# Loading all of x first and summing the adaptive columns in five groups

## The chip, the cores and the metric

The kernel runs on one core of one Trainium2 chip. The core has five engines with an instruction queue each: TensorE (PE; its weight loads are shown as PEld), VectorE (DVE), ScalarE (ACT), GpSimd (POOL) and SyncE (SP), which issues the DMAs. Each engine takes its own instructions strictly in the order in which they are written, and waits for the others through semaphores. The metric is the device time of one execution in microseconds. The times shown are the median of three runs.

## The reference, cut to what matters

Two layers of a decoder trunk run on x, 1024 rows (positions) by 1024 channels. Each layer begins with a norm of x that is scaled and shifted per channel, and then multiplies by the columns of a projection:

```python
c_act = jax.nn.silu(c)
for l in range(DEPTH):
    ada = c_act @ w_ada[l] + b_ada[l]
    shift, scale, gate = jnp.split(ada, 3, axis=-1)
    h = rmsnorm(x, norm_g[l]) * (1.0 + scale[:, None, :]) + shift[:, None, :]
    p = h @ w_in[l]
    ...                       # mLSTM heads and retention heads on the columns of p
    x = x + gate[:, None, :] * (concat(y_m, y_r) @ w_out[l])
return rmsnorm(x, final_g)
```

`w_ada[l]` is 1024 by 3072. The change touches layer 0 alone, and of it only what stands here up to the first columns of `p`.

## The kernel before, in words

Matrix products are made in three passes for accuracy: each operand is split into a rounded high part and a low part, and `mm3` (lines 144 to 147) multiplies high by high, low by high and high by low. So each 128 x 128 weight tile costs three matmuls of 512 columns for each half of the rows.

Everything ahead of the value projection of layer 0 is the first stage. It is written out by hand for all engines (lines 1052 to 1181), as a list of steps in a string, `script`; the kernel's scheduler takes over behind it for the engines other than TensorE, whose order is written throughout. The stage makes the products of the normed x with three column blocks of 128 (`firsts`), for 8 blocks of 128 channels (k) and 2 halves of 512 rows. Each pair (half, k) is a number n in `seq`, and passes through these steps:

- `T`: four transposes on TensorE of the scaled x (line 315) into one PSUM bank of the pool `pa`, which has four; one is kept for the adaptive sums and two, once in use, for the third weight's products, so that in most of the stage one is left for `T`
- `E`: evacuation with the channel's scale and shift (`gsh`), on ACT at line 321 or on VectorE at line 323
- `C`: the high part, a cast on ACT (line 1137)
- `U`: the low part, a subtraction on VectorE (line 1140)
- `F`: the nine matmuls with the three weights (lines 145 to 147)

The scale and the shift of a channel come out of `w_ada`. `ada_load` (line 232) loads a group of columns in eight pieces of 128 rows; step `A` (lines 244 and 246, VectorE) multiplies each piece by its entry of silu(c) and adds it up; step `P` (line 251, TensorE) sums over the partitions by four matmuls with a column of ones, each shown as two records; step `G` (lines 227 to 230, VectorE) makes `gsh` of them, with the columns of `norm_g` and `b_ada` that `ada_cols` (lines 193 to 199) has transposed on TensorE and copied on VectorE. There are four groups of 256 channels; a group's `E` waits for its `G`.

Of the other steps, `S` and `Q` are the squares of x's first and second half (ACT and VectorE in turn, lines 1072 and 1069) and, with `R`, the reciprocal root (POOL, line 1013); `N` and `X` scale the two halves (ACT line 308, VectorE line 310), step 0 for the first four channel blocks and steps 1 and 2 for the rest; `W` splits a weight (cast on ACT, line 614, subtraction at line 615: on POOL for the weights' first halves, `W00 W10 W20`, and on VectorE for the second); `D` multiplies a mask by itself on TensorE, and nobody reads the result (line 1151); `V` splits the weights of the value projection.

All loads are issued by SP in the order of lines 1082 to 1096. Eight semaphores take turns among the DMAs, so each issue waits until the DMA eight places ahead has landed. The order before is: c, the rows of `norm_g` and `b_ada`, adaptive group 0, x's first half, the first halves of three weights, x's second half, groups 1 and 2, the weights' second halves, group 3, then what comes later. `load_cact`, `ada_cols` and all of group 0's `A` stand ahead of the script.

Of the kernel before, what the change touches and what calls it, by code (L numbers as in the profile page):

```python
# [19 lines left out]
P = 128  # L20

D = 1024
# [58 lines left out]
def tile_hybrid_trunk(ctx, tc, x, c, positions, w_ada, b_ada, norm_g, w_in, conv_w, conv_b,  # L81
# [149 lines left out]

    def ada_load(l, g):
        raws = []
        for kk in range(KT):
            raw = bt()
            Q.dma_start(raw.rearrange("p (w c) -> p w c", w=2),
                        w_ada[l, kk * P:(kk + 1) * P].rearrange("p (w c) -> p w c", c=D)[:, 0:2, g * 256:(g + 1) * 256])
            raws.append(raw)
        return raws

    def ada_group(raws, acc, kks):
        for kk in kks:
            if kk == 0:
                V.tensor_scalar(acc, raws[0], cact[:, 0:1], None, ALU.mult)
            else:
                V.scalar_tensor_tensor(acc, raws[kk], cact[:, kk:kk + 1], acc, ALU.mult, ALU.add)

    def ada_sums(l, g, acc, pt):
        for which in range(2):
            for i in range(2):  # L250
                PE.matmul(pt[:, 4 * g + 2 * which + i:4 * g + 2 * which + i + 1],
                          acc[:, which * 256 + i * P:which * 256 + (i + 1) * P], ones, start=True, stop=True)
# [307 lines left out]
    def ocol(hg, m):  # L560
        return OFF_MO + hg * HD + m * P
# [537 lines left out]
    ada_cols(0, arows)  # L1099
    accs = [bt()]  # L1100
    ada_group(araw[0], accs[0], range(KT))
    pad = ps_a()

    for l in range(DEPTH):
# [8 lines left out]
        def first(half, k):  # L1113
            for i, w in enumerate(wf):
                if k == 0:
                    pf[i][half] = ps_p() if i < 2 else ps_a()
                half_block(pf[i][half], w, hT, half, k, k + 1)

        if l == 0:
            seq = [(half, k) for g in range(4) for half in range(2) for k in (2 * g, 2 * g + 1)]  # L1120
            w0, pts, hfs, rs1 = [], {}, {}, []
            script = ("P0 D6 S G0 W00 W10 N0 W20 T0 T1 E0 E1 C0 C1 U0 U1 F0 F1 Q R A102 X0 A124 T2 E2 C2 A146 T3 D3 E3 C3 U2 F2 "
# [4 lines left out]
            for step in script.split():  # L1127
# [4 lines left out]
                elif what == "E":  # L1132
                    hfs[n] = norm_evac(0, pts.pop(n), seq[n][1], n >= 2)
# [7 lines left out]
                elif what == "F":  # L1141
                    first(*seq[n])
                elif what == "A":
# [3 lines left out]
                    ada_group(araw[g], accs[g], range(a, b))  # L1147
                elif what == "D":
                    warm = ps_a()
# [4 lines left out]
                elif what == "G":  # L1154
                    finish_gsh(0, 2 * n, 2, pad[:, 4 * n:4 * n + 2], pad[:, 4 * n + 2:4 * n + 4])
# [21 lines left out]
                else:  # L1177
                    i, p = (int(d) for d in arg)
                    wf[i] += split_w(rw[i][p], P, V if p else G)
            head_cols(0, hrows)  # L1180
            startup.__exit__(None, None, None)
        else:
            for half in range(2):
                for k in range(KT):
                    first(half, k)
                    tick()
# [110 lines left out]
```

## Time and profile before

| | us |
|---|---|
| median of three runs | 2311.66 |
| lowest and highest | 2311.54, 2311.84 |
| the profiled execution's own time | 2311.88 |
| span of its records | 2310.0 |
| TensorE busy | 2277.8 (99%) |
| VectorE busy | 1353.2 (59%) |
| ACT busy | 907.1 (39%) |
| POOL busy | 823.5 (36%) |

How to read the lines below. In order of time: start, duration, engine, line, operation, output<-inputs, shape, x count of merged records; in brackets the idle time of that engine just before and what ended it. In a group of instructions: count | busy time, mean ns of one | idle time before them and what ended most of it. In a table of stretches: start and end, length, then busy time of each engine with the number of its instructions, the granted clock of TensorE as a share of full speed, the busy share of the DMA engines, and GB/s. A matmul on 32-bit floats (`T`, `P`, `D`, line 197) is shown as two records. The profile is of one execution.

### The profile page before, as it was taken

How to read it: one execution, taken by the hardware profiler on the slowest of the kernel's cores; microseconds unless marked ns; L12 is line 12 of the kernel's file. 1: busy time of each engine (PE TensorE's matmuls, PEld its weight loads, DVE VectorE, ACT ScalarE, POOL GpSimd, SP SyncE). 2: the span in 40 equal slices, each digit the busy share in tenths (PEclk: the TensorE clock that was granted, in tenths of full speed). 3: DMA queues.
4: the chain of work that ended last, by engine and by line, in shares of the span. 5: the costliest groups of instructions: out<-in, count | busy, mean ns of one | idle time of the engine just before them, and what ended most of it. 6: DMA issues, size and time to landing. Idle time of an engine off the chain costs nothing.

```text
span 2310.0 us, 34281 instructions
## 1 busy us (share of the span) xinstructions
PE 2277.8 (99%) x12447; PEld 1958.2 (85%) x12447; DVE 1353.2 (59%) x2835; ACT 907.1 (39%) x1768; POOL 823.5 (36%) x817
## 2 busy tenths in 40 slices
PE   7999999999999999999999999999999999999998
PEld 5888888889988888888888889888898888988886
DVE  7477688556555555584536665555563545556753
ACT  5535433444332323353434544344443323224442
POOL 1343424333343334222552434233334334341323
PEclk9999999999999999999999999999999999999999
DMA  8223232324433533486532322322323333436762
GB/s 257 80 64 98 73 84 80 82 74 116 120 109 88 150 83 87 128 258 217 177 92 57 84 72 77 84 74 69 81 70 89 81 87 93 124 81 205 240 231 78
DMA packets 328761, 259.44 MB, mean 112 GB/s; under 512 B 79732, under 2 KB 263804, under 8 KB 328592
## 3 DMA queue, kind: packets, MB, share of 16 engines
q1 hardware_dynamic: 328592, 257.27, 38.6%
q8 instruction: 97, 1.59, 0.3%
q14 instruction: 72, 0.59, 0.1%
HBM read 201.58 MB, written 55.61 MB: 111 GB/s over the span
## 4 chain that ended last, share of the span: by engine, by line
PE 91%; DVE 3%; DMA 3%; issue 1%; POOL 1%; ACT 1%; SPq 0%; POOLq 0%; DVEq 0%; ACTq 0%
PE pp L145 24%; PE pp L146 24%; PE pp L147 24%; PE pa L146 5%; PE pa L147 5%; PE pa L145 5%; PE pa L765 2%; DMA b<-in_w_ada_dram 1%; DMA b<-in_x_dram 1%; PE pa L315 0%; DMA raw<-in_w_ada_dram 0%; POOL wL L615 0%; POOL sL L615 0%; DVE b L266 0%; DMA b<-in_w_in_dram 0%
## 5 line engine op out<-in xcount | busy, mean ns | idle before, releaser
L145 PE MATMUL pp<-b,wH 128*128 128x512 f32 x1776 | 703.7, 396 | 1.1 <-ACT b L1137 1.1
L146 PE MATMUL pp<-b,wH 128*128 128x512 f32 x1776 | 700.2, 394 | 0.3 <-DVE b L1140 0.2
L147 PE MATMUL pp<-b,wL 128*128 128x512 f32 x1776 | 700.2, 394 | 0.0
L615 POOL TENSOR_TENSOR wL<-raw,wH 128x512 fp32r<-128x512 f32 x338 | 450.1, 1338 | 507.4 <-ACT wH L614 466.8
L147 PEld LDWEIGHTS pp<-b,wL 128*128 128x128 f32 x1776 | 333.9, 188 | 79.0
L146 PEld LDWEIGHTS pp<-b,wH 128*128 128x128 f32 x1776 | 334.2, 188 | 72.2 <-DVE b L1140 2.0
L145 PEld LDWEIGHTS pp<-b,wH 128*128 128x128 f32 x1776 | 334.4, 188 | 71.5 <-ACT b L1137 1.6
L614 ACT CAST wH<-raw 128x512 fp32r<-128x512 f32 x402 | 246.1, 616 | 322.8 <-PE pp L147 93.8
L145 PE MATMUL pp<-wH,b 128*128 128x256 f32 (+1 forms) x1152 | 353.0, 306 | 0.7 <-DVE g L543 0.7
L147 PE MATMUL pp<-wH,b 128*128 128x256 f32 (+1 forms) x1152 | 352.8, 306 | 0.0
L146 PE MATMUL pp<-wL,b 128*128 128x256 f32 (+1 forms) x1152 | 352.2, 306 | 0.0
L615 POOL TENSOR_TENSOR b<-acc,b 128x256 fp32r<-128x256 f32 (+1 forms) x208 | 200.8, 984 | 322.8 <-ACT b L614 315.2
L145 PEld LDWEIGHTS pp<-wH,b 128*128 128x128 f32 x1152 | 216.9, 188 | 12.3 <-DVE g L543 1.6
L147 PEld LDWEIGHTS pp<-wH,b 128*128 128x128 f32 x1152 | 216.6, 188 | 11.4
L146 PEld LDWEIGHTS pp<-wL,b 128*128 128x128 f32 x1152 | 216.7, 188 | 10.8
L632 DVE SCALAR_TENSOR_TENSOR acc<-pp,cols,acc 128x511 f32<-128x511 f32 (+2 forms) x192 | 142.5, 742 | 43.2 <-ACT acc L627 41.2
L614 ACT CAST b<-acc 128x256 fp32r<-128x256 f32 (+1 forms) x208 | 93.7, 487 | 187.4 <-DVE acc L709 127.6
L615 POOL TENSOR_TENSOR sL<-th,sH 128x384 fp32r<-128x384 f32 (+1 forms) x64 | 61.0, 953 | 236.5 <-ACT sH L614 171.9
L145 PE MATMUL pa<-wH,b 128*128 128x512 f32 x256 | 101.1, 395 | 0.0
L147 PE MATMUL pa<-wH,b 128*128 128x512 f32 x256 | 101.0, 394 | 0.0
L146 PE MATMUL pa<-wL,b 128*128 128x512 f32 x256 | 100.9, 394 | 0.0
L636 ACT ACTIVATE th<-acc 128x512 f32<-128x512 f32 x64 | 40.5, 632 | 146.3 <-DVE acc L634 79.3
(255 smaller groups left out, 3439.3 us busy)
## 6 DMA issues: line engine op xcount, KB each, us to landing
raw<-in_w_in_dram SPq DMA_DIRECT2D x274, 256.0 KB
raw<-in_w_out_dram SPq DMA_DIRECT2D x128, 256.0 KB
gdr<-g SPq DMA_DIRECT2D x64, 256.0 KB
ndr<-zt SPq DMA_DIRECT2D x128, 128.0 KB
raw<-in_w_ada_dram SPq DMA_DIRECT2D x64, 256.0 KB
g<-gdr SPq DMA_DIRECT2D x64, 256.0 KB
acc<-ndr SPq DMA_DIRECT2D x64, 256.0 KB
acc<-kdr SPq DMA_DIRECT2D x192, 64.0 KB
```

Of the source, the lines that this page charges most:

```text
L145: PE.matmul(o, lt[0], rt[0], start=start, stop=False)
L146: PE.matmul(o, lt[0], rt[1], start=False, stop=False)
L147: PE.matmul(o, lt[1], rt[0], start=False, stop=stop)
L614: A.copy(dst[0], src)
L615: eng.tensor_tensor(dst[1], src, f(dst[0]), ALU.subtract)
L632: V.scalar_tensor_tensor(acc[:, d:], pt[:, 0:HALF - d], wcol, acc[:, d:], ALU.mult, ALU.add)
L636: A.activation(th, acc, AF.Tanh, scale=0.5)
L765: PE.matmul(pd, kk[i][:, o:o + P], qd, start=dt == 0 and i == 0, stop=dt == 1 and i == 1)
```

## The change

The order of loads becomes: c, all of x, the rows of `norm_g` and `b_ada`, two weights' first halves, group 0, the third weight's first half, groups 1, 2 and 3, the weights' second halves, group 4. The groups are of 1, 1, 2, 2 and 2 blocks of 128 channels. For a group of one block, two pieces of `w_ada` share a buffer and are loaded by a DMA each, of half the size; its sums are over 256 columns instead of 512, and its `P` has two matmuls. The numbers n follow the groups: 0 and 1 are k = 0 of both halves, 2 and 3 are k = 1, and from 4 on they are as before.

The script is written anew. The squares and the scaling of both halves, two transposes and the warm-up multiplies (eight instead of six, and the later three go) stand ahead of `ada_cols`, now step `L`, and of group 0's `A`. For n = 0 and 1 the products with the first two weights (`f00 f01 f10 f11`) are written ahead of those with the third (`f02 f12`). A group's `A` is written about half a step earlier than before, and `P3 G3` ahead of `W01 W11 W21`. All weights are split on POOL, and all `E` run on ACT.

```diff
+    GROUPS = ((0, 1), (1, 1), (2, 2), (4, 2), (6, 2))
+
     def ada_load(l, g):
+        k, n = GROUPS[g]
         raws = []
-        for kk in range(KT):
+        for kk in range(0, KT, 3 - n):
             raw = bt()
-            Q.dma_start(raw.rearrange("p (w c) -> p w c", w=2),
-                        w_ada[l, kk * P:(kk + 1) * P].rearrange("p (w c) -> p w c", c=D)[:, 0:2, g * 256:(g + 1) * 256])
-            raws.append(raw)
+            for i in range(3 - n):
+                part = raw[:, i * 256:(i + 1) * 256] if n == 1 else raw
+                Q.dma_start(part.rearrange("p (w c) -> p w c", w=2),
+                            w_ada[l, (kk + i) * P:(kk + i + 1) * P].rearrange("p (w c) -> p w c", c=D)
+                            [:, 0:2, k * P:(k + n) * P])
+                raws.append(part)
         return raws
...
     Q.dma_start(crow[0:8, :], c[0].rearrange("(r c) -> r c", c=P))
+    xts = [load_x(0), load_x(1)]
     arows = load_ada_rows(0)
+    firsts = (zcol(0, 0), ocol(0, 0), zcol(0, 1))
+    rw = [[w_raw(col, 0)] for col in firsts[0:2]]
     araw = [ada_load(0, 0)]
-    xts = [load_x(0)]
-    firsts = (zcol(0, 0), ocol(0, 0), zcol(0, 1))
-    rw = [[w_raw(col, 0)] for col in firsts]
-    xts.append(load_x(1))
-    araw.append(ada_load(0, 1))
-    araw.append(ada_load(0, 2))
+    rw.append([w_raw(firsts[2], 0)])
+    araw += [ada_load(0, g) for g in (1, 2, 3)]
     for i, col in enumerate(firsts):
         rw[i].append(w_raw(col, 1))
-    araw.append(ada_load(0, 3))
+    araw.append(ada_load(0, 4))
...
     load_cact(crow)
-    ada_cols(0, arows)
-    accs = [bt()]
-    ada_group(araw[0], accs[0], range(KT))
+    accs = []
...
-            seq = [(half, k) for g in range(4) for half in range(2) for k in (2 * g, 2 * g + 1)]
-            script = ("P0 D6 S G0 W00 W10 N0 W20 T0 T1 E0 E1 C0 C1 U0 U1 F0 F1 Q R A102 X0 A124 T2 E2 C2 A146 T3 D3 E3 C3 U2 F2 "
-                      "A168 U3 P1 G1 N1 T4 F3 E4 C4 U4 N2 A202 T5 F4 E5 C5 U5 X1 A224 T6 F5 E6 C6 U6 X2 A246 T7 F6 E7 C7 "
-                      "A268 U7 W01 W11 W21 P2 G2 T8 F7 E8 C8 A302 U8 T9 F8 E9 C9 A324 U9 T10 F9 E10 C10 A346 U10 T11 F10 "
-                      "E11 C11 A368 U11 P3 G3 T12 F11 E12 C12 U12 T13 F12 V0 E13 C13 V1 U13 T14 F13 E14 C14 V2 U14 "
-                      "T15 F14 E15 C15 V3 U15 V4 F15 V5 V6 V7")
+            seq = [(half, k) for k0, n in GROUPS for half in range(2) for k in range(k0, k0 + n)]
+            script = ("S N0 T0 T2 D8 Q R L W00 W10 A003 X0 T1 A038 P0 G0 E0 C0 E1 C1 W20 A102 U0 f00 A124 f01 A146 U1 f10 f11 "
+                      "A168 P1 A201 G1 f02 f12 E2 C2 T3 E3 C3 A213 U2 N1 T4 F2 A236 A268 U3 P2 G2 F3 A302 N2 E4 C4 U4 "
+                      "T5 F4 E5 C5 A324 U5 X1 T6 F5 E6 C6 A346 U6 X2 T7 F6 E7 C7 A368 U7 P3 G3 W01 W11 W21 T8 F7 E8 C8 "
+                      "A402 U8 T9 F8 E9 C9 A424 U9 T10 F9 E10 C10 A446 U10 T11 F10 E11 C11 A468 U11 P4 G4 T12 F11 "
+                      "E12 C12 U12 T13 F12 V0 E13 C13 V1 U13 T14 F13 E14 C14 V2 U14 T15 F14 E15 C15 V3 U15 V4 F15 V5 V6 V7")
...
+                elif what == "f":
+                    first(*seq[n // 10], n % 10)
+                elif what == "L":
+                    ada_cols(0, arows)
...
-                    wf[i] += split_w(rw[i][p], P, V if p else G)
+                    wf[i] += split_w(rw[i][p], P)
```

In the script, `A124` is group 1's pieces 2 and 3; `f01` is n = 0 with weight 1; `D8` is eight warm-up multiplies.

More of the change, by code (lines that the diff above doesn't have):

```diff
@@ L248, in ada_sums @@
     def ada_sums(l, g, acc, pt):
+        k, n = GROUPS[g]
         for which in range(2):
-            for i in range(2):
-                PE.matmul(pt[:, 4 * g + 2 * which + i:4 * g + 2 * which + i + 1],
-                          acc[:, which * 256 + i * P:which * 256 + (i + 1) * P], ones, start=True, stop=True)
+            for i in range(n):
+                o = which * KT + k + i
+                PE.matmul(pt[:, o:o + 1], acc[:, (which * n + i) * P:(which * n + i + 1) * P], ones, start=True, stop=True)
     def ada_rows(l, c0, accs):
@@ L1141, in tile_hybrid_trunk @@
                 elif what == "F":
-                    first(*seq[n])
+                    for i in range(3):
+                        first(*seq[n], i)
+                elif what == "f":
+                    first(*seq[n // 10], n % 10)
+                elif what == "L":
+                    ada_cols(0, arows)
                 elif what == "A":
@@ L1184, in tile_hybrid_trunk @@
                 for k in range(KT):
-                    first(half, k)
+                    for i in range(len(wf)):
+                        first(half, k, i)
                     tick()
```

23 lines of the change are left out of this document (12 added, 11 removed).

## The prediction

> **What bounds the kernel now.** I read the page first, then busy time by stretch, then the first 74 us in order of time, by engine, with each wait. The stretches say where a gain can lie at all. Columns: PE, PEld, DVE, ACT, POOL busy (instructions), granted clock, DMA share, GB/s.
>
> ```profile
> span 2310.0 us, 34281 instructions
> 24.41:40.49 16.08, 15.57 (x65) 12.13 (x66) 12.82 (x30) 10.52 (x21) 1.19 (x1) 0.82 1.11 351
> 40.49:73.96 33.47, 32.49 (x167) 25.83 (x166) 22.82 (x39) 24.20 (x49) 6.62 (x12) 1.00 0.27 80
> 73.96:170.00 96.04, 96.04 (x515) 82.20 (x514) 58.32 (x117) 43.38 (x79) 37.70 (x38) 1.00 0.31 74
> 170.00:2300.00 2130.00, 2123.07 (x11669) 1830.51 (x11669) 1239.83 (x2611) 817.68 (x1599) 770.10 (x753) 1.00 0.38 110
> ```
>
> From 73.96 us on, where the first stage ends, TensorE is idle for 7 us in 2226. Nothing there gives slack back, so the end moves by as much as the first stage's end. All that counts is when TensorE finishes that stage. Its rows up to the first product, and the granted clock around it:
>
> ```profile
> 12.73 1.86 PE L251 MATMUL pa<-ones,b 128*128 128x1 f32 x8 [8.90 <-DVE b L246]
> 14.46 5.47 PE L1151 MATMUL pa<-rmask 128*128 128x256 f32 x12
> 22.52 0.77 PE L315 MATMUL pa<-ident,b 128*128 128x128 f32 x5 [0.97 <-DVE b L310]
> 24.41 0.79 PE L145 MATMUL pp<-b,wH 128*128 128x512 f32 x1 [1.12 <-ACT b L1137]
> 27.43 0.63 PE L145 MATMUL pa<-b,wH 128*128 128x512 f32 x1
> 27.86 0.63 PE L146 MATMUL pa<-b,wH 128*128 128x512 f32 x1
> 32.97 1.56 PE L1151 MATMUL pa<-rmask 128*128 128x256 f32 x6 [0.43 <-ACT acc L321]
> 36.80 0.95 PE L251 MATMUL pa<-ones,b 128*128 128x1 f32 x8
> 23.00:23.50 0.50, 0.29 (x3) 0.05 (x1) 0.50 (x1) 0.00 (x0) 0.50 (x1) 0.85 1.06 389
> 30.00:30.50 0.50, 0.50 (x3) 0.46 (x2) 0.37 (x2) 0.23 (x1) 0.24 (x1) 0.82 1.10 348
> ```
>
> The first product starts at 24.41. The clock is half from about 23.35 (0.85 over half a microsecond is 1.0 for 0.35 and 0.5 for 0.15) to 30.18 (0.82, in the same way): 6.83 us, two periods of 3.41. Counted back, further borders lie at 19.94, 16.52 and 13.11, and the next at 33.59. The warm-up multiplies of step D show as 12 records in 5.47 us at 14.46, 0.456 each, against 0.26 each at 32.97, so they ran slow to their end although the clock column says 1.00 there; I go by the durations. The full clock thus came at 19.94, just as they ended, and was lost at 23.35. [...]
>
> **The change, part by part.** *Loads.* The bytes are the same: group 0 and group 1 become 8 loads of 128 KB each, 512 bytes a piece, instead of 8 of 256 KB; 8 issues are added on SP's queue. The whole of x goes ahead of everything but c and the constants.
>
> ```profile
> 1.64 0.28 SPq L178 DMA_DIRECT2D rows<-in_norm_g_dram  x1
> 2.30 3.98 SPq L236 DMA_DIRECT2D b<-in_w_ada_dram  x8
> 5.08 0.49 DVE L244 TENSOR_SCALAR b<-b,cact 128x512 f32<-128x512 f32 x1 [0.96 <-DMA b<-in_w_ada_dram]
> 10.50:16.50 6.00, 3.77 (x13) 3.42 (x14) 4.01 (x9) 2.17 (x6) 0.00 (x0) 1.00 1.05 380
> 16.50:20.00 3.50, 3.42 (x9) 2.16 (x7) 1.80 (x10) 2.35 (x5) 1.49 (x2) 1.00 1.13 328
> 17.25 0.69 DVE L1069 SCALAR_TENSOR_TENSOR th<-b 128x512 f32<-128x512 f32 x1 [0.71 <-ACT th L1072]
> 19.57 1.33 ACT L308 ACTIVATE b<-b,rs 128x512 f32<-128x512 f32 x2
> ```
>
> x takes the place of the row at 1.64. The first load was used 2.78 us after its issue (2.30 to 5.08); the rest follow by 262 KB at 380 GB/s, 0.69 us, a little slower at the start, so 0.72: the eighth load of the first half lands at 1.64 + 2.78 + 7 x 0.72 = 9.5, the sixteenth at about 15. Two weight loads end near 16.7, group 0 (1.05 MB at the 328 GB/s of the stretch that has such 512-byte pieces in it) near 20, then a weight load, and group 1 near 25: SP issued eight in 3.98 us, so 0.5 each is its own bound. Groups 2 and 3 follow near 31 and 37, group 4 near 45. Each is there before it is asked for below, by 5 us or more for group 0's last load, so the smaller loads cost nothing; without that cover they would cost 16 x (0.5 - 0.4), under 2 us.
>
> *Ahead of the first product.* The order is now: norm of x's first half, two transposes T0 and T2, eight warm-up multiplies instead of six, then L, the transposition of the norm_g and b_ada rows, which in the kernel before stood ahead of all this. TensorE works in order, so L waits for all of D8; VectorE works in order too, and L's two copies stand ahead of all of group 0's sums, of the scaling X0 and of everything behind. This is the wait that the change adds. From the last square to the scaling took 2.32 us (17.25 to 19.57): here 9.5 to 11.8. Two scalings on ACT, 1.33, give 13.15; six transposes more (five took 0.77) end at 14.1. D8 is 16 records: 7.3 us at 0.456. At the border of 19.94, 12.8 of them are done; the other 3.2 at half the time end at **20.7**. From there the path is VectorE's:
>
> ```profile
> 3.54 0.28 PE L197 MATMUL pa<-ident,rows 32*128 32x32 f32 x1 [0.53 <-DMA rows<-in_b_ada_dram]
> 3.94 0.17 DVE L199 COPY cols<-pa 128x24 f32<-128x24 f32 x1
> L244 DVE TENSOR_SCALAR b<-b,cact 128x512 f32<-128x512 f32 x4 | 1.9, 482 | 1.0 <-DMA b<-in_w_ada_dram 1.0
> L246 DVE SCALAR_TENSOR_TENSOR b<-b,cact,b 128x512 f32<-128x512 f32 x28 | 21.0, 750 | 2.3 <-DMA b<-in_w_ada_dram 1.7
> L818 DVE SCALAR_TENSOR_TENSOR cf<-cf,pa 128x256 f32<-128x256 f32 x64 | 25.6, 401 | 0.0
> 30.27 0.88 DVE L310 TENSOR_SCALAR b<-b,rs 128x512 f32<-128x512 f32 x2
> 37.78 0.16 DVE L227 TENSOR_TENSOR gsh<-pa,cols 128x2 f32<-128x2 f32 x1 [0.94 <-PE pa L251]
> 38.30 0.78 ACT L321 ACTIVATE acc<-pa,gsh 128x512 f32<-128x512 f32 x1 [2.16 <-PE pa L315]
> 39.11 0.62 ACT L1137 CAST b<-acc 128x512 fp32r<-128x512 f32 x1
> 39.76 0.69 DVE L1140 TENSOR_TENSOR b<-acc,b 128x512 fp32r<-128x512 f32 x1 [1.56 <-ACT b L1137]
> ```
>
> L to its copies' end, 3.54 to 4.11: 0.57, so 21.3. Group 0 is one 128x256 TENSOR_SCALAR (0.28, a good half of 0.48) and seven 128x256 sums at 0.41 (the nearest row has 0.40; half of 0.75 is the lower end), with X0's two scalings, 0.88, among them: 4.0, so 25.3. Its sums on TensorE are four records at the slow 0.23 of the row at 12.73, since the clock is lost again at 23.35: 0.95, so 26.3. From there as from 37.78 to the end of the cast, 39.73: 1.95. The first product starts at **28.25**, 3.85 later than before, and TensorE is idle for some 6 of the 7.5 us ahead of it.
>
> *From the first product to the fifth step's (F4).* The products of group 0 use two weights; the third weight's come after group 1's sums. The second record of the first product waits for VectorE's 0.69, so 28.95; eleven at the slow 0.43 (27.43 to 27.86 above) end at 33.7, about when the border at 33.59 gives the clock back. Group 1's sums, small vectors and evacuation (0.5, 0.5, 0.8) end at 35.55, with the six products of the third weight beside them; T3, E3 and T4 wait for one another through one PSUM slot (0.45, 0.15, 0.8, 0.45), F2 runs from 37.5 to 39.6. VectorE has from 34.75 on two sums of group 2, one U, and five sums: 1.55 + 0.7 + 3.87, so 40.9; group 2's sums on TensorE wait for that, 1.3 us idle. F3 then ends at 43.85, T5 at 44.3. Before, 24.41 to 40.49 was 16.1; now 28.25 to 44.3 is 16.05: nothing won back. The warm-up D3 that went (1.56) is paid for by these waits.
>
> *From F4 to the stage's end.* The transposes mark the steps:
>
> ```profile
> 42.69 0.60 PE L315 MATMUL pa<-ident,b 128*128 128x128 f32 x4
> 45.21 0.60 PE L315 MATMUL pa<-ident,b 128*128 128x128 f32 x4
> 48.66 1.05 PE L251 MATMUL pa<-ones,b 128*128 128x1 f32 x8 [0.75 <-DVE b L246]
> 49.57 0.63 PE L315 MATMUL pa<-ident,b 128*128 128x128 f32 x4
> 52.27 0.66 PE L315 MATMUL pa<-ident,b 128*128 128x128 f32 x4
> 55.59 0.60 PE L315 MATMUL pa<-ident,b 128*128 128x128 f32 x4
> 49.12 1.89 DVE L615 TENSOR_TENSOR wL<-b,wH 128x512 fp32r<-128x512 f32 x3
> L615 POOL TENSOR_TENSOR wL<-raw,wH 128x512 fp32r<-128x512 f32 x338 | 450.1, 1338 | 507.4 <-ACT wH L614 466.8
> ```
>
> A step is 2.52 (42.69 to 45.21), nine products at 0.23 and four transposes; a group's sums (36.80) take 0.82 more, until the next transposes. Between 45.21 and 55.59 stand three steps and one such sum: 8.4, but they took 10.4. These 2.0 us were lost to group 2's last VectorE sums, to the three weight splits of 1.89 on VectorE and to the evacuation behind them. In the new order the next group's sums start half a step earlier and are reduced ahead of the splits, and the splits lie on POOL (three of 1.34, about 4 us, beginning some 2 us ahead of the first product that needs them, and the last needed 4 us later): I take the 2.0 as won. The rest, 33.47 - 2.0, brings the end from 44.3 to **75.8**, 1.8 behind 73.96. The first two evacuations move from VectorE to ACT, at 0.78 (38.30); VectorE's nearest row, U's 0.69, bounds what that costs at 0.1 each, and E1 lies beside the first products.
>
> Sum: +3.85 - 0.05 - 2.0 = +1.8 on the profiled execution's 2311.88, which stands 0.22 above the median: 2311.66 + 1.8 = **2313.5**. Unknown prices: D8's end between 18.9 and 21.4; the 2.0 won between 0.5 and 2.0.
>
> **Rivals.** [...]
>
> [...]
>
> *The loads decide (slower by over 0.2%).* If the 512-byte pieces of groups 0 and 1 move at a third of 328 GB/s, group 1 ends near 37 instead of 25, and its sums on TensorE, due at 33.7, come at 37.4: +3.7 more, **2317.2**. It decides from below 2.36 MB in the 16.5 us from 16.7 to 33.2, 145 GB/s; the stretch with such pieces shows 328.
>
> *The change does what its order suggests.* Were the rows' copies not behind D8, group 0 would be summed by 20.6 and the first product would start at 23.3 on a warm clock, with the 2.0 won as well: 23.3 + 42 us of TensorE work + 2.5 of waits = 67.8, **2305.5**. Against it: both engines keep their order.
>
> **How the numbers follow.** Forecast 0.5, earlier clock 0.25, slower clock 0.14, loads 0.05, no wait 0.06. The predicted time is the forecast's. The range from 2309.6 to 2316.2 takes in the first three with their bounds, and leaves out the last two. A measurement of this kernel can tell about 0.2%, 4.6 us, from no change. By that the first three are no change but for the slower clock's upper part (0.05); with the loads, slower is 0.10, faster 0.06, the same 0.84.
>
> **What the changed profile would show.** D's 16 records from about 14.1 to 20.7; VectorE idle from about 16 until the copies of the rows; the first product near 28, slow until about 33.6; the step F4 near 44; no wait of over 0.3 us from there to the stage's end near 75.8; TensorE full behind it. Wrong it would be by a first product ahead of 26.5 or behind 29.5, by the 2.0 us staying, or by waits behind the first stage that are not in the profile of before.

## The result, and the profile after

The changed kernel takes 2318.06 us (median of nine runs, 2315.56 to 2320.13). The kernel before, run beside it, takes 2311.81 (2311.46 to 2312.56). The ratio is 1.0026, with a 95% interval from 1.0016 to 1.0037: slower by 6.2 us, which is 0.26%, where 1.8 us were forecast, and outside the range that ended at 2316.2.

The profiled execution took 2318.66 us. Its parts, beside those of the kernel before and of the forecast ("F4" is the moment at which the step F4 begins, behind the transposes T5):

| us | before | forecast | after |
|---|---|---|---|
| first product | 24.41 | 28.25 | 29.01 |
| from there to F4 | 16.08 | 16.05 | 17.33 |
| from F4 to the stage's end | 33.47 | 31.47 | 33.10 |
| stage's end | 73.96 | 75.8 | 79.44 |
| profiled time less stage's end | 2237.9 | 2237.9 | 2239.2 |

TensorE in order of time in the kernel after (a file line here is eight above its number in the kernel before; L323 is T, L1160 is D, L197 the step L, L260 is P, L206 the first record behind the stage; the row at 42.93 is P2, group 2's sums; a transposition of T or L is one record here, a matmul of P or D two):

```profile
16.11 4.33 PE L1160 MATMUL pp<-rmask 128*128 128x256 f32 x16
20.38 0.25 PE L197 MATMUL pa<-ident,rows 32*128 32x32 f32 x1
25.99 0.98 PE L260 MATMUL pa<-ones,b 128*128 128x1 f32 x4 [2.24 <-DVE b L253]
29.01 0.80 PE L145 MATMUL pp<-b,wH 128*128 128x512 f32 x1 [2.03 <-ACT b L1141]
33.20 0.80 PE L146 MATMUL pp<-b,wH 128*128 128x512 f32 x1 [0.53 <-DVE b L1144]
42.93 1.05 PE L260 MATMUL pa<-ones,b 128*128 128x1 f32 x8 [0.20 <-DVE b L253]
45.99 0.60 PE L323 MATMUL pa<-ident,b 128*128 128x128 f32 x4
51.24 0.60 PE L323 MATMUL pa<-ident,b 128*128 128x128 f32 x4
54.58 0.63 PE L323 MATMUL pa<-ident,b 128*128 128x128 f32 x4
57.13 0.60 PE L323 MATMUL pa<-ident,b 128*128 128x128 f32 x4
59.14 0.50 PE L146 MATMUL pp<-b,wH 128*128 128x512 f32 x1 [1.17 <-DVE b L1144]
61.11 0.60 PE L323 MATMUL pa<-ident,b 128*128 128x128 f32 x4
79.44 0.25 PE L206 MATMUL pa<-ident,rows 96*128 96x96 f32 x1
```

Two things stand out. The first product waits in a chain from 20.38 to 29.01. And the step from T9 (57.13) to T10 (61.11) takes 3.98 instead of 2.52, because the second matmul of a product waits 1.17 for VectorE's low part. VectorE and POOL of the same kernel, in the same view, say what VectorE did meanwhile (L1077 is a square, L198 the copy of the rows, L251 and L253 the adaptive sums, L1144 a low part U; on POOL, L623 is a weight's low part):

```profile
11.08 0.69 DVE L1077 SCALAR_TENSOR_TENSOR th<-b 128x512 f32<-128x512 f32 x1 [1.80 <-DMA b<-in_x_dram]
20.66 0.17 DVE L198 COPY cols<-pa 128x8 f32<-128x8 f32 x1 [2.84 <-PE pa L197]
20.84 0.70 DVE L251 TENSOR_SCALAR b<-b,cact 128x256 f32<-128x256 f32 x1
23.28 2.56 DVE L253 SCALAR_TENSOR_TENSOR b<-b,cact,b 128x256 f32<-128x256 f32 x5
27.35 0.35 DVE L251 TENSOR_SCALAR b<-b,cact 128x256 f32<-128x256 f32 x1
29.60 2.94 DVE L253 SCALAR_TENSOR_TENSOR b<-b,cact,b 128x256 f32<-128x256 f32 x4
44.36 0.48 DVE L251 TENSOR_SCALAR b<-b,cact 128x512 f32<-128x512 f32 x1
44.87 0.75 DVE L253 SCALAR_TENSOR_TENSOR b<-b,cact,b 128x512 f32<-128x512 f32 x1
55.20 1.60 DVE L251 TENSOR_SCALAR b<-b,cact 128x512 f32<-128x512 f32 x1
56.83 1.66 DVE L253 SCALAR_TENSOR_TENSOR b<-b,cact,b 128x512 f32<-128x512 f32 x1
...
18.88 2.50 POOL L623 TENSOR_TENSOR wL<-b,wH 128x512 fp32r<-128x512 f32 x2
30.89 1.37 POOL L623 TENSOR_TENSOR wL<-b,wH 128x512 fp32r<-128x512 f32 x1 [9.50 <-ACT wH L622]
53.99 3.95 POOL L623 TENSOR_TENSOR wL<-b,wH 128x512 fp32r<-128x512 f32 x3 [21.73 <-ACT wH L622]
```

At four places a VectorE instruction beside a subtraction of POOL takes 1.4 to 3.3 times as long as the same instruction without one: 0.70 against 0.35 (20.84 and 27.35), 0.73 each, in the mean of four, against 0.51 (29.60 and 23.28), 1.60 against 0.48 (55.20 and 44.36), 1.66 against 0.75 (56.83 and 44.87). That is the lead for the experiments. The granted clock and the stretches behind it, with the columns of the prediction's table:

```profile
24.00:24.50 0.50, 0.00 (x0) 0.00 (x0) 0.46 (x2) 0.00 (x0) 0.00 (x0) 0.88 0.94 265
38.00:38.50 0.50, 0.50 (x3) 0.33 (x2) 0.38 (x2) 0.26 (x1) 0.00 (x0) 0.96 1.10 326
29.01:46.34 17.33, 15.73 (x60) 11.79 (x61) 13.95 (x27) 8.43 (x13) 1.37 (x1) 0.74 1.10 345
46.34:79.44 33.10, 31.93 (x167) 25.93 (x166) 22.35 (x35) 23.97 (x48) 10.53 (x15) 1.00 0.18 46
```

The clock is half from 24.38 to 38.04, which is 13.66 us, against 6.83 in the kernel before. Behind the stage TensorE is full, as before: it is busy for all of the 90.56 us from 79.44 to 170.00.

### The profile page after: what moved, and what is told of

It reads as the page before. It is cut to its first block, busy times and chain, and to the rows that moved or that the text cites. A ratio compares the mean times of both kernels' runs of the same rounds, so it can differ in the third digit from the quotient of the medians.

```text
span 2316.9 us, 34307 instructions
## 1 busy us (share of the span) xinstructions
PE 2276.4 (98%) x12445; PEld 1959.0 (85%) x12445; DVE 1356.6 (59%) x2841; ACT 909.2 (39%) x1770; POOL 827.1 (36%) x820
## 4 chain that ended last, share of the span: by engine, by line
PE 55%; DVE 1%; POOL 1%; issue 0%; DMA 0%; ACT 0%; POOLq 0%; DVEq 0%; ACTq 0%
PE pp L145 14%; PE pp L147 14%; PE pp L146 14%; PE pa L146 4%; PE pa L147 4%; PE pa L145 4%; PE pa L773 1%; POOL b L623 0%; DMA raw<-in_w_in_dram 0%; PE pa L323 0%; DVE b L318 0%; DMA raw<-in_w_out_dram 0%; DVE th L1005 0%; DVE wL L623 0%; DVE acc L640 0%
## 5 line engine op out<-in xcount | busy, mean ns | idle before, releaser
L623 POOL TENSOR_TENSOR wL<-raw,wH 128x512 fp32r<-128x512 f32 x338 | 451.3, 1342 | 506.3 <-ACT wH L622 473.4
L623 POOL TENSOR_TENSOR b<-acc,b 128x256 fp32r<-128x256 f32 (+1 forms) x208 | 199.9, 981 | 324.0 <-ACT b L622 308.9
L623 POOL TENSOR_TENSOR sL<-th,sH 128x384 fp32r<-128x384 f32 (+1 forms) x64 | 60.6, 947 | 238.5 <-ACT sH L622 173.0
```

Of the source, the lines that this page charges most:

```text
L623: eng.tensor_tensor(dst[1], src, f(dst[0]), ALU.subtract)
```

## The experiments

*Theory.* POOL's subtractions hold up VectorE's instructions beside them; the change put them beside the sums that everything waits for. *Rivals:* the wait behind D8, the half clock, the order of loads, or a VectorE that is simply full. Measured, all on one scale (T8 to T11 are three steps, 7.6 us when nothing waits; a profile is one execution, the median is of 5 to 11 runs, and each ratio is to the kernel before in the same set of runs, whose medians were 2311.81 to 2312.80):

| kernel | first product | T8 to T11 | stage's end | median | ratio to before, interval |
|---|---|---|---|---|---|
| before | 24.41 | 8.54 | 73.96 | 2311.81 | |
| after | 29.01 | 9.05 | 79.44 | 2318.06 | 1.0026 [1.0016, 1.0037] |
| after again | 29.57 | 9.09 | 80.08 | 2317.51 | 1.0021 [1.0012, 1.0030] |
| rows ahead of D8 | 27.75 | 9.12 | 78.25 | 2315.90 | 1.0016 [1.0007, 1.0025] |
| second splits on VectorE | 29.74 | 8.74 | 79.86 | 2317.22 | 1.0021 [1.0012, 1.0030] |
| both of these | 28.36 | 8.74 | 78.47 | 2315.88 | 1.0013 [1.0005, 1.0022] |
| more warm-up multiplies | 28.38 | 9.11 | 78.91 | 2319.29 | 1.0030 [1.0019, 1.0042] |
| x behind group 0 | 23.68 | 9.85 | 88.46 | 2326.88 | 1.0060 [1.0046, 1.0074] |
| no low parts | 28.35 | 7.62 | 76.32 | 2315.07 | 1.0011 [1.0002, 1.0020] |
| after, all on VectorE | 27.26 | 8.83 | 75.13 | 2314.02 | 1.0010 [1.0001, 1.0019] |
| the same, third low part earlier | 27.02 | 8.23 | 75.70 | 2313.75 | 1.0007 [0.9998, 1.0016] |
| before, splits on POOL | 24.47 | 9.33 | 74.82 | 2313.49 | 1.0003 [0.9995, 1.0012] |
| before, first splits on VectorE | 23.12 | 8.55 | 74.28 | 2310.70 | 0.9995 [0.9986, 1.0004] |
| before, second splits spread | 24.51 | 9.94 | 75.44 | 2313.98 | 1.0009 [1.0000, 1.0017] |
| before, both | 22.66 | 9.95 | 73.94 | 2312.53 | 1.0003 [0.9994, 1.0012] |
| before, both, casts early | 23.21 | 8.23 | 72.78 | 2311.71 | 0.9996 [0.9987, 1.0005] |
| the same, with D5 | 22.91 | 8.23 | 73.19 | 2312.25 | 0.9999 [0.9990, 1.0008] |

The profiled time less the stage's end lies between 2237.4 and 2240.2 in all of them, without regard to the edit. So the 1.3 us that the kernel after lost behind the stage lie within what differs from one execution to the next, and where two medians are within 2 us I go by the stage's end and its waits. The stage's end itself differs between executions, by 0.64 us between the two profiles of the kernel after.

**No low parts.** To see what POOL's subtractions cost, this run leaves them out:

```diff
-                    wf[i] += split_w(rw[i][p], P)
+                    wH = wt("wH", 512, 6, F32R)
+                    A.copy(wH, rw[i][p])
+                    wf[i] += [(wH[:, a * P:(a + 1) * P], wH[:, a * P:(a + 1) * P]) for a in range(4)]
```

> The changed kernel without the low parts of the three weights in the first stage: POOL's six subtractions are left out and the matmuls take the high part in their place (so the products lack the low parts of these weights). TensorE's work is the same. Theory (VectorE's instructions last up to three times as long beside POOL's subtractions, and this delays the sums of groups 0 and 1 and the step T9 to T10): the 128x256 TENSOR_SCALAR falls from 0.70 to about 0.35 us, four sums at 29.6 us from 2.94 to about 2.0, the 128x512 pair at 55.2 us from 1.60 and 1.66 to 0.48 and 0.75; first product near 28.2, T9 to T10 2.5 us, stage's end near 76 us, time 2314 to 2315 us. Rival (they are slow because of the DMA loads that land at the same time, or of the waits): the durations stay, only the matmuls' wait for the low part goes, stage's end 78.5 or later, time 2317 us or more.

VectorE in order of time, and the two stretches ahead of the stage's end:

```profile
20.53 0.35 DVE L251 TENSOR_SCALAR b<-b,cact 128x256 f32<-128x256 f32 x1
28.94 2.04 DVE L253 SCALAR_TENSOR_TENSOR b<-b,cact,b 128x256 f32<-128x256 f32 x4
53.40 0.48 DVE L251 TENSOR_SCALAR b<-b,cact 128x512 f32<-128x512 f32 x1
53.91 0.75 DVE L253 SCALAR_TENSOR_TENSOR b<-b,cact,b 128x512 f32<-128x512 f32 x1
```

```profile
28.35:44.68 16.33, 14.55 (x60) 11.05 (x61) 13.05 (x27) 8.43 (x13) 0.00 (x0) 0.81 1.10 344
44.68:76.32 31.64, 31.64 (x167) 25.94 (x166) 20.30 (x35) 23.87 (x48) 6.58 (x12) 1.00 0.22 60
```

Every disputed duration is back at its undisturbed value while the loads go on as before, which rules out the loads. TensorE has no idle time left in the second stretch. The stage ends 3.1 us earlier (0.66 ahead of the first product, 1.00 in the stretch to F4 and 1.46 behind it), and the median is 2.4 us below that of the unchanged kernel run beside it. The theory holds. The edit also takes away the matmuls' waits for the weights' low parts, but in this stage of the kernel after no wait of TensorE ended on POOL. Not all of the 3.1 us need be POOL's: 0.3 of the 0.66 is D8, which ended earlier in this execution (VectorE's copies begin at 20.36 instead of 20.66), and this profile, at 2313.86 us, is the fastest of the 11 runs, 1.2 below their median.

**Splits on POOL in the kernel before** does that part of the change alone:

```diff
-                    wf[i] += split_w(rw[i][p], P, V if p else G)
+                    wf[i] += split_w(rw[i][p], P)
```

> The kernel before with this one part of the change: the splits of the weights' second halves on POOL. Theory 'POOL's splits slow VectorE': group 3's first VectorE sums beside them take 1.6 each, and the time grows by 0.5 to 1.5 us over 2311.8 or, since VectorE is rid of 1.89 us of splits, stays. Rival 'the move is a gain', as the prediction took it: it falls by 0.5 to 2 us.

POOL's three took 4.69 us from 48.08, and VectorE beside them did this:

```profile
48.59 1.76 DVE L1140 TENSOR_TENSOR b<-acc,b 128x512 fp32r<-128x512 f32 x1
50.52 1.01 DVE L230 TENSOR_TENSOR gsh<-sm,cols 128x2 f32<-128x2 f32 x1
51.46 1.60 DVE L244 TENSOR_SCALAR b<-b,cact 128x512 f32<-128x512 f32 x1
```

The U of 0.69 takes 1.76, a vector of two columns 1.01 instead of 0.16. T8 to T11 grows from 8.54 to 9.33. What the prediction took as a gain is a loss of 0.8 us in this stage, and of 1.1 us in the median beside that of the kernel before in the same set of runs (2312.42).

**Second splits on VectorE** undoes that part in the kernel after (`split_w(rw[i][p], P, V if p else G)`).

> The changed kernel with the splits of the weights' second halves back on VectorE. In the changed kernel, while POOL makes them (53.99 to 57.94), a VectorE TENSOR_SCALAR of 0.48 takes 1.60 and a sum of 0.75 takes 1.66, and the step behind is 1.46 longer than 2.52. Theory 'POOL's splits slow VectorE': both come back to their usual length, the step loses 0.5 to 1.4 us of its excess (VectorE now has 1.9 us of splits instead), and the time falls by about 1 us. Rival 'the excess is the evacuation's own chain': the step stays at about 4.0 and the time within 0.3 us, or longer.

It brings back 0.3 us in the step T9 to T10, less than the 0.5 to 1.4 of the theory: three low parts in a row, 1.89 us at 55.81, delay U instead. The engine alone isn't the matter; where the work lies counts too.

**Rows ahead of D8**, and **both** edits together:

```diff
-"S N0 T0 T2 D8 Q R L W00 W10 A003 ..."
+"S N0 T0 T2 Q R L D8 W00 W10 A003 ..."
```

> The changed kernel with L (the rows' transposition and its two copies) written ahead of D8 instead of behind it; nothing else. In the changed kernel VectorE's copies start at 20.66, 2.84 us after it went idle, and group 0's sums end at 25.84. Theory 'VectorE waits behind the warm-up': the sums follow the landing of group 0 (5.8 MB at the rates of the stretches, near 20.5) and end at 21.3, the first product starts near 24.4 instead of 29.0, and the time falls by 3 to 5 us from 2318.1 to 2313 to 2315. Rival 'the loads set the start': group 0 lands late, the sums end no earlier than 24.5, and the time falls by less than 1.5 us.

> The changed kernel with two parts undone together: the transposition of the norm_g and b_ada rows (L) stands ahead of the warm-up multiplies D8, and the second halves of the three weights are split on VectorE. Theory (two separate losses, one at the start of the chain and one in the step T9 to T10): they add up, the single edits having given 2.2 us and 0.8 us, so about 2315.0 us, the stage's end near 77.5 us. Rival (both edits only relieve the same VectorE queue, and one of them is enough): no better than the first alone, 2315.9 us, stage's end near 78.3.

```profile
16.97 0.28 PE L197 MATMUL pa<-ident,rows 32*128 32x32 f32 x1 [0.91 <-DMA rows<-in_b_ada_dram]
27.75 0.73 PE L145 MATMUL pp<-b,wH 128*128 128x512 f32 x1 [2.03 <-ACT b L1141]
...
18.54 0.35 DVE L251 TENSOR_SCALAR b<-b,cact 128x256 f32<-128x256 f32 x1 [0.83 <-DMA b<-in_w_ada_dram]
19.07 2.65 DVE L253 SCALAR_TENSOR_TENSOR b<-b,cact,b 128x256 f32<-128x256 f32 x2 [0.17 <-DMA b<-in_w_ada_dram]
```

L is free at 16.97, 3.4 us earlier than in the kernel after, but the first product comes only 1.3 earlier: the sums now start at 18.54, when group 0's loads land, and the two at 19.07 take 2.65 instead of 1.0 beside POOL. Of the 1.3, 0.4 are the clock, which was still full when group 0's sums ran on TensorE (0.58 us against 0.98). So the wait behind D8 is real, and costs at most a third of what it seems to. With both edits together the stage ended no earlier (78.47 against 78.25) and the median was the same. This doesn't decide for that run's rival: T8 to T11 did shorten, from 9.12 to 8.74, but the first product came 0.61 later, ahead of anything that the second edit touches.

**More warm-up multiplies.** They fill TensorE's idle stretches ahead of the first product (`D5` behind T1, `D4` behind P0).

> The changed kernel with TensorE's idle time ahead of the first product filled: five warm-up multiplies behind T1 and four behind group 0's sums; nothing depends on them. In the changed kernel the clock is half from 24.38 to 38.02. Theory 'the cold clock costs, and its border wanders': the clock stays full, the products up to 38 take half as long, VectorE's chain becomes the bound, the time falls by 1.3 to 2.5 us, and the runs lie closer together than 4.6 us. Rival 'VectorE's chain is the bound already': less than 0.5 us.

```profile
40.92 1.05 PE L260 MATMUL pa<-ones,b 128*128 128x1 f32 x8 [0.98 <-DVE b L253]
42.50:43.00 0.50, 0.50 (x3) 0.39 (x2) 0.46 (x2) 0.47 (x1) 0.00 (x0) 0.50 1.09 361
```

The clock stayed at 1.00 from 20 to 42.50 us, and P2 began 2.0 us earlier than in the kernel after (40.92 instead of 42.93), 0.6 of it already at the first product. But then the clock was half all the same, until about 45.9 (products of 0.63 us up to the one at 44.83, of 0.48 from 45.94 on), and the products F3 took 3.41 us (41.84 to 45.25) instead of 2.15. The stage ended at 78.91, only 0.5 earlier, and the median was no better. So this run doesn't rule the clock out: the half clock moved, and took back much of what the full one had won.

**x behind group 0** undoes the load order and keeps the five groups:

```diff
-    xts = [load_x(0), load_x(1)]
     arows = load_ada_rows(0)
+    araw = [ada_load(0, 0)]
+    xts = [load_x(0)]
...
-"S N0 T0 T2 D8 Q R L W00 W10 A003 X0 T1 A038 P0 G0 E0 C0 E1 C1 W20 ..."
+"L A008 P0 D8 S G0 W00 W10 N0 T0 E0 C0 W20 U0 f00 f01 f02 Q R X0 T1 E1 C1 ..."
```

> The changed kernel with its load order undone and its five groups kept: rows, group 0 (8 loads of 128 KB), x's first half, two weights' first halves, x's second half, the third weight, groups 1 to 3; L and all of group 0's sums stand first in the script, and the products n = 0 with all three weights come before n = 1. Theory (the first product is late because the loads of x stand ahead of group 0, so that VectorE's sums lie behind the norm; the groups of 128 channels are harmless): group 0's sums end near 9 us, the first product starts at 18 to 20 us, n = 1 waits for x's second half until about 24, and the stage ends at 70 to 73 us, time 2308 to 2311 us. Rival (VectorE's sums, squares and low parts between 18 and 45 us are as many as before and set the end of the stage whatever comes first): the early products only bring more waits, the stage ends at 74 us or later, time 2312 us or more.

The first product did come earlier, at 23.68, but n = 1 needs x's second half, whose scaling began at 29.50, so that its first product came at 33.10, and group 3's sums came so late that TensorE was idle for 3.57 us ahead of them:

```profile
23.68 0.79 PE L145 MATMUL pp<-b,wH 128*128 128x512 f32 x1 [1.52 <-ACT b L1142]
61.01 1.87 PE L260 MATMUL pa<-ones,b 128*128 128x1 f32 x8 [3.57 <-DVE b L253]
```

The stage ended 9 us later than in the kernel after. My theory failed here: with groups of one channel block n = 1 already needs x's second half, and undoing the load order alone is worse than either kernel. How much of the 9 us is the load order isn't shown, since the script was written anew with it, the rest of group 3's sums directly ahead of P3, and since the last two of these sums took 3.44 us at 57.52, beside POOL, instead of 1.53.

**After again.** The unchanged kernel, beside the last ones.

> The changed kernel itself once more, unchanged, beside the others: 2317 to 2319 us. It tells how far the other three can be read, and whether the 4.6 us between its lowest and highest time come from the first stage (theory: the borders of the clock window lie elsewhere in each execution, so its end moves by a microsecond or two) or from behind it (rival: the stage's end is within 0.5 us of 79.4 and the rest differs from 2239.2 us).

```profile
42.12 1.05 PE L260 MATMUL pa<-ones,b 128*128 128x1 f32 x8 [0.99 <-DVE b L253]
26.50:27.00 0.50, 0.39 (x3) 0.42 (x3) 0.00 (x0) 0.00 (x0) 0.00 (x0) 0.67 0.90 282
43.50:44.00 0.50, 0.50 (x4) 0.37 (x3) 0.50 (x2) 0.27 (x1) 0.00 (x0) 0.74 1.11 352
```

Stage's end 80.08, behind it 2238.6: neither part repeats to 0.5 us, and the 4.6 us between the changed kernel's lowest and highest time aren't put down to one of them. But the clock's borders do lie elsewhere, as the theory has it: the same kernel now has the half clock from 26.67 to 33.5 and again from 43.74 to about 47.1 (a product takes 0.63 us at 45.99, and 0.49 at 47.12), where the first profile had it from 24.38 to 38.04. P2 began 12.55 us behind the first product instead of 13.92, and F3 then took 3.38 us instead of 2.15. And D8 ended at 21.4 instead of 20.4, so that group 0's sums began behind POOL's first two subtractions and weren't held up by them: from L to their sums on TensorE it took 5.26 us instead of 5.61.

**First splits on VectorE in the kernel before.** If the theory is right, the kernel before has the same stall ahead of its own first product. Here `w` is a weight's cast alone and `W` its low part, on VectorE:

```diff
-"P0 D6 S G0 W00 W10 N0 W20 T0 T1 E0 E1 C0 C1 U0 U1 F0 F1 Q R ..."
+"P0 D6 S G0 w00 W00 w10 N0 W10 w20 T0 T1 E0 E1 C0 C1 U0 U1 W20 F0 F1 Q R ..."
```

> The kernel before with the low parts of the weights' first halves on VectorE instead of POOL: that of the first weight ahead of the scaling N0, in a wait of 0.82 us, that of the second behind it, that of the third behind U1. In the kernel before the two scalings at 19.57 take 2.90 us beside POOL's 4.09 us of such subtractions, against 0.88 for the two at 30.27. Theory (VectorE's instructions are held up by POOL's beside them): the two scalings fall to 0.88 us, T1 ends some 2 us earlier, the first product starts at 22.4 to 22.9 instead of 24.41, and as VectorE takes over 1.9 us of work, about 1 us of it remains at the stage's end: near 73.0, time about 2311.3 us. Rival (the scalings are slow for another reason, such as ACT's or the loads): they stay at 2.9 us, the first product moves to 25 us or later, time 2313 us or more.

VectorE's scalings, TensorE's D3, and the granted clock:

```profile
18.90 0.69 DVE L1188 TENSOR_TENSOR wL<-b,wH 128x512 fp32r<-128x512 f32 x1
19.74 0.88 DVE L310 TENSOR_SCALAR b<-b,rs 128x512 f32<-128x512 f32 x2
...
32.02 2.46 PE L1152 MATMUL pa<-rmask 128*128 128x256 f32 x6 [0.43 <-ACT acc L321]
...
32.50:33.00 0.50, 0.50 (x3) 0.37 (x3) 0.50 (x1) 0.50 (x2) 0.00 (x0) 0.53 1.09 379
```

The two scalings fall from 2.90 to 0.88 and the first product comes 1.3 us earlier, at 23.12, somewhat less than the theory says. But TensorE was then idle for 2.04 us, the clock went to half at 32.53, D3 took 2.46 instead of 1.56, and nothing of the gain was left at the stage's end. That holds for this execution, whose 2312.32 us lie 1.6 above the median of the 11 runs; for the faster ones there is no profile.

**Second splits spread, and both edits.** In the kernel before, one low part goes beside P2, one ahead of U8 and one behind it:

```diff
-"A268 U7 W01 W11 W21 P2 G2 T8 F7 E8 C8 A302 U8 ..."
+"A268 U7 P2 W01 G2 T8 F7 E8 C8 W11 U8 W21 A302 ..."
```

> The kernel before with the low parts of the weights' second halves still on VectorE, but spread: one while TensorE makes group 2's sums, one ahead of U8 and one behind it, where the kernel before has the three in a row ahead of P2. Theory (the prediction's reading that 2.0 us between 45.21 and 55.59 were lost to these three in a row holds, only POOL was the wrong place for them): P2 moves from 48.66 to about 47.9, the step to T9 to about 2.6 us, stage's end 72.0 to 73.0, time 2310.5 to 2311.5 us. Rival (VectorE is full there, and what is taken out of one wait comes back in the next): stage's end 73.7 or later, time 2312 us or more.

> The kernel before with both edits: no weight of the first stage is split on POOL, the first halves' low parts lie in VectorE's waits around N0, the second halves' are spread. Theory: the two gains add up, stage's end 71 to 72.5, time 2309.5 to 2311 us, ahead of both kernels. Rival (VectorE full): no more than the better of the two single edits.

Both theories failed: T8 to T11 grew to 9.94 and 9.95. VectorE wasn't full, though. It stood idle for 2.08 us ahead of the second low part, because I had left that weight's cast on ACT behind C8.

**The places settled.** What was still open: whether VectorE is full between T8 and T11, or the places were badly chosen, and whether the clock ate the gain of the earlier first product. First the kernel after with L ahead of D8 and all nine low parts on VectorE (`Q R w00 W00 w10 W10 L D8`, `P1 W20 A201 G1`, `w01 w11 w21 U7 P3 W01 G3 T8 F7 E8 C8 W11 U8 W21 A402`); then three more runs: the kernel before with both edits and the casts early (`w01 w11 w21 U7 P2 W01 G2 T8 F7 E8 C8 W11 W21 U8 A302`), the same with `D5` ahead of T2, and the kernel after with `W11 W21 U8 A402`. The 3.74 us that the texts below call T9 to T10 were the step T10 to T11 in that run.

> The changed kernel with the transposition of the rows ahead of D8, and the low parts of all nine weight blocks on VectorE, placed in its waits (the first two ahead of the rows' copies, the third while TensorE makes group 1's sums, the second halves while it makes group 3's and around U8). Theory (what the change lost is the late first product, of which POOL's subtractions and the wait behind D8 are parts, and the step T9 to T10): first product at 26 to 27.5, T9 to T10 under 3 us, stage's end 74.5 to 76.5, time 2312.3 to 2314.3 us, ahead of the changed kernel by 3 us or more and about level with the kernel before. Rival (the chain from x to group 0's sums is bound by the loads, which lie behind x): first product at 27.5 or later, time 2315 us or more.

> The kernel before without any split on POOL in the first stage, as in the run of both edits, but the casts of the second halves stand ahead of U7, and their low parts one beside group 2's sums on TensorE and two ahead of U8, in the wait for its cast (2.08 us idle there in the run with the spread alone). Theory (it was the places): T9 to T10 at most 2.9 us, the stage's end 72.3 to 73.5 us, time 2310 to 2311.5 us. Rival (VectorE is full there): T9 to T10 3.3 us or more, the stage's end 73.9 or later, time 2312 us or more.

> The same as the run before it with five warm-up multiplies more, between the products F1 and the transposes T2, where TensorE is idle for 2.04 us. Theory (the half clock after that idle stretch ate the gain of the earlier first product: the six multiplies of D3 took 2.46 instead of 1.56 us and the products behind them ran at half speed for 1.6 us): clock full from 20 us on, T4 at 36.5 instead of 37.9, the stage's end 1 us or more ahead of the run without, time 2309 to 2310.5 us. Rival (VectorE's sums of group 1 set T4): T4 and the stage's end within 0.4 us of the run without.

> The changed kernel as in the last run of it (rows ahead of D8, all low parts on VectorE in its waits), with the third weight's second low part ahead of U8 instead of behind it. Theory (the place): T9 to T10 falls from 3.74 to at most 3.0 us, the stage's end to 74.2 to 74.8, time 2313.0 to 2313.6 us. Rival (VectorE full): 3.5 us or more, stage's end 75 or later, time 2314 us or more.

VectorE in the kernel before with both edits and early casts:

```profile
48.27 0.69 DVE L1188 TENSOR_TENSOR wL<-b,wH 128x512 fp32r<-128x512 f32 x1
49.23 1.29 DVE L1188 TENSOR_TENSOR wL<-b,wH 128x512 fp32r<-128x512 f32 x2
```

T9 to T10 is 2.54 in both kernels with the new places, T8 to T11 8.23; the stage of the kernel before ends 1.2 us earlier, at 72.78. So it was the places, except for 0.6 us that are left in T10 to T11. The time, 0.9996 [0.9987, 1.0005], can't be told from the kernel before: a stage's end 1.2 us earlier is below what these runs separate. D5 decided nothing: in both of its kernels the half clock happened to fall from about 24.3 to 27.7, so there was no half clock behind F1 to prevent, and D5 only added 0.4 us to T4.

The kernel after gains most: 75.13 and 75.70 for the stage's end, medians 2314.02 and 2313.75, some 4 us below the changed kernel. Of the two, the one with the better places ends 0.6 later, and misses the 74.2 to 74.8 of its theory. Its granted clock shows why: with all instructions the same up to there, it goes to half at 39.61, behind the wait for group 2's sums, and F3 takes 3.72 us (39.51 to 43.23) where the other run's took 2.16.

```profile
39.50:40.00 0.50, 0.50 (x4) 0.40 (x4) 0.28 (x3) 0.00 (x0) 0.00 (x0) 0.61 1.20 297
```

## Why the prediction was wrong

**The direction of the sum held, its size did not.** First product later, order a little better behind F4, stage's end later: all as forecast. Of the 3.7 us between the forecast parts and 79.44, the first product is 0.76, the stretch to F4 1.28, and the rest of the stage 1.63.

**The step that failed** is "the splits lie on POOL ... I take the 2.0 as won". The prediction asked whether POOL would be in time, and it was; it did not ask what POOL would do to VectorE. Of the 2.0, the part lost to group 2's late sums did go: T7 to T8 was 4.36 before (45.21 to 49.57) and is 3.34 after (51.24 to 54.58). The part lost to the splits did not: T9 to T10 went from 3.32 to 3.98, which is 1.46 above a step that waits for nothing. So 0.4 us were won from F4 to the stage's end (33.47 to 33.10), not 2.0. The same subtractions stretched the sums of groups 0 and 1, which the prediction priced as if undisturbed, by 0.35 and 0.90. Without POOL's work the two stretches took 16.33 and 31.64 us, against 16.05 and 31.47 forecast, and the first product came at 28.35 against 28.25.

How much of the 3.7 us is POOL's is known within bounds. The 1.46 and the 0.35 are read off their rows, together 1.8. What the 0.90 cost isn't separated from the half clock: in after again these sums were as long (2.94; the low part behind them is used 4.19 us behind the first product in both), but the clock was back at 33.5, and P2 began 12.55 us behind the first product, about as forecast (40.9 less 28.25). So POOL accounts for 1.8 to 2.7 of the 3.7 us, and the medians with and without its work differ by 2.4.

The row that would have told it stood in the trace of before, beside POOL's three subtractions:

```profile
19.57 2.90 DVE L310 TENSOR_SCALAR b<-b,rs 128x512 f32<-128x512 f32 x2 [0.82 <-POOL rs L1013]
19.50 4.09 POOL L615 TENSOR_TENSOR wL<-b,wH 128x512 fp32r<-128x512 f32 x3
```

The same two scalings took 0.88 at 30.27. The prediction quoted that row, and of 19.57 only ACT's two scalings, so it did not ask why VectorE's differ.

The 1.60 and 1.66 beside POOL are VectorE's own 0.48 and 0.75 plus 1.12 and 0.91, each less than one subtraction (1.32, a third of 3.95). If each of the six subtractions held one VectorE instruction for the 1.34 us of the prediction's row, that would be 8 us, my estimate of the most; the stretched rows of the kernel after were longer by 3.3 us in all (0.35, 0.90, 1.12 and 0.91). By what way POOL's work holds VectorE's up, no run here shows.

**x lands at 9.5** fell short: the last square of x's first half could start at 11.08 only. In this execution it cost nothing, by luck: D8 began 2.0 us later than forecast but still ended at 20.4 (forecast 20.7), since the border of the clock lay at 17.56 (6.83 us ahead of 24.38), and not at 19.94: its records last 0.63 us up to the one at 16.97, and 0.38 from 17.70 on. In after again D8 ended at 21.4 and the first product came at 29.57.

**The clock's borders** were taken from one profile of the kernel before, and don't carry over. A half clock lasts 3.41 us in two of the runs (32.53 to 35.94 with the first splits on VectorE, 39.61 to 43.02 in the last one), and two, three or four times that in others (6.83 before, 10.24 without low parts, 13.66 after); in after again the second one begins 10.24 behind the end of the first (33.5 to 43.74). Counted in periods of 3.41 from the start, the border lies at 2.9 in the kernel before, at 0.5 in the kernel after, at 2.8 in the same kernel run again, at 1.8 and 2.1 in the runs that lost the clock at 32.53 and 39.61. So the kernel doesn't fix it, though three runs of before agree within 0.3 us (2311.54 to 2311.84). The forecast's sum uses 19.94 and 33.59 as borders of the changed kernel, and no run shows that it keeps them: its clock came back at 38.04 and, run again, at 33.5. In the kernel after, the half clock thus lasted 4.4 us longer than forecast, and P2 began 13.92 us behind the first product instead of the 12.65 forecast; with the clock back at 33.5 it was 12.55. This is the rest of what failed in the stretch to F4. An execution that got its clock back early paid elsewhere: from P2 to T5 it is 3.06 us in the kernel after, and 4.29 and 4.33 in after again and in the run with more warm-up multiplies, which lost the clock in F3.

**Group 0's 128x256 sums at 0.41** took 0.51 each undisturbed (2.56 for five), as its scalar one took 0.35 instead of 0.28: together some 0.8 us on the way to the first product, beside POOL's 0.35.

**The rivals.** The earlier clock, at 0.25, came true in part: the border lay 2.4 us earlier than the forecast's, but D8 also began 2.0 later, and ended only 0.3 earlier. No run shows the 18.9 that bounds D8's end from below, nor which work of TensorE brings the full clock: where D8 kept its place it ended between 20.14 (no low parts) and 21.54 (second splits on VectorE). The slower clock, at 0.14, came true in part as well: the half clock ended at 38.04 instead of 33.59, but D8 had sped up at 17.56. The rival of no wait behind D8 would have had the first product at 23.3 if that wait went; with the wait gone it came at 27.75, bound by group 0's loads and POOL. In the kernel after, the smaller loads decided nothing. The 2.0 came out at 0.4, just below its bounds (0.5 to 2.0 won): its part from group 2's sums was won, and for the move to POOL a loss was not considered.

**What remains of the loss** when POOL is out of it: in the kernel after with all low parts on VectorE the first product still comes 2.6 to 2.9 us later than before, since group 0's sums lie behind both halves of x instead of under their loads, and the better order behind it gave back 1.7 or 0.9 of it, by where the clock fell: the stage ends at 75.13 or 75.70, against 73.96. Against the kernel before with the same care for the low parts, which ends the stage at 72.78, these are 2.4 and 2.9 us more.

## What to carry to other kernels

When work moves to an engine that is idle, look for the same instruction in the trace with and without that engine busy beside it: two rows with the same shape and different durations are a price list. This stage of short dependent steps lost more by a stretched instruction in its chain than by the same low parts placed in VectorE's waits (with the rows ahead of D8 it ended at 78.25 with the low parts on POOL, and at 75.13 and 75.70 with them on VectorE). And the clock border seen in one execution was not a property of the kernel (0.5 and 2.8 in two executions of the same one); a sum that leans on it needs both cases.

## What the hardware showed that was not expected

- A VectorE instruction on 128x2 elements took 1.01 us instead of 0.16 beside POOL's subtractions: a stall of 0.85 us, where the instruction's own work is 0.16.
- Loads of 128 KB are issued about 0.5 us apart, and with them the traffic falls to 265 GB/s at 24 us, against 389 at 23 us in the kernel before; no chain in the kernel after ended on it.
- The same instructions in the same order, up to there, lost the full clock in one execution and kept it in another (F3 in 3.72 or 2.16 us), and in the two profiles of the kernel after the half clock lay at 24.38 to 38.04, and at 26.67 to 33.5 and 43.74 to about 47.1.
